# Eighteen more tiles turned by transposing transfers in a two-layer transformer trunk

## The chip, the cores and the metric

The kernel runs on one core of a Trainium2 chip. The metric is device time in microseconds (us) of one execution, as the median of several runs. One further execution was recorded by the profiler; all lines of the profile are from it.

## The reference

Two layers work on one residual stream `x` of 256 tokens by 2048 features, in f32. Layer 0 has differential attention, layer 1 multi-head latent attention. Each layer then attends into 256 memory tokens and applies a squared-ReLU MLP of width 8192:

```
mem_h = rms_norm(mem, mem_norm)
for i in range(2):
    h = rms_norm(x, attn_norm[i])
    x = x + (diff_attention(h) if i == 0 else mla_attention(h))
    x = x + memory_cross_attention(rms_norm(x, cross_norm[i]), mem_h, ...)
    x = x + square(relu(rms_norm(x, mlp_norm[i]) @ wup)) @ wdown
return rms_norm(x, final_norm)
```

Differential attention has 16 query and 16 key heads of 128 features, rotated in their first 32 features. Two softmaxes are subtracted for each of 8 pairs, the result weights values of 256 features, and each head's result is normed.

## The kernel before

**Tiles.** The 256 tokens are two row tiles (t = 0, 1) of 128 partitions. Features are handled in chunks of 512. TensorE contracts over partitions, so whatever enters a product as the stationary or contracted side must lie with features on partitions. Results come out with tokens on partitions. Between two products a 128x512 tile is therefore turned, as four 128x128 squares.

**Precision.** Every f32 operand is kept as a high and a low half (`hi`, and `lo = x - hi`), and each product is made of three matmuls: hi by hi, hi by lo, lo by hi. Weights arrive as 1 MB raw tiles (`raw_tile`, 7 buffers) by loads that SP issues in program order. ScalarE casts the high half (`whi`, L221), VectorE subtracts the low half (`wlo`, L222). One raw tile gives 24 matmuls. `take` keeps four raw tiles asked for ahead.

**Two ways to turn a tile.** On TensorE: `transpose4` calls `flip` (L174) four times into PSUM; `split` then makes the halves (ScalarE L366, VectorE L367). By transfers: `half_words` (L375) has ScalarE copy the 16-bit halves of the words into two planes (L377) and GpSimd (POOL) store them to DRAM (L379); `turned_by_dma` (L382) has SP issue a transposing transfer back into SBUF (L384), in program order with the weight loads; `split_landed` makes the halves from the tile that landed (L390, L391). Before the change the second way is used for MLP blocks 1 to 6 of each layer, four tiles a block, 48 in all.

**Order.** TensorE's order is written out by hand. Work beside the weight products (turning, softmax, scores) is written as generators, `Task`. A task yields a number: the time after which its next piece is due, by a clock that the program advances with each matmul that it emits (`mmul`, `flip`). `pump`, called behind every few matmuls, emits the pieces that are due. `need` emits whatever a product still waits for. So the constants T_EV to T_DMA, in us, say how long a piece is expected to take. ScalarE, VectorE and POOL get their order from a scheduler that simulates the timeline; `keep_in_program_order` ties single instructions to the written order: weight loads and transposing transfers on SP, accumulating loads on POOL, and the cast in `split_landed` on ScalarE.

**Differential attention.** `attention` goes through four groups of four heads. `project_diff(gi)` makes queries, keys and values of a group, each a chunk product of four raw tiles. `heads_T` (L568) evacuates queries or keys (L550), rotates them on POOL (`rope`, L561 to L566) and turns them. `attend_diff` is started when the group's values are made, and its pieces run under the next group's products; `normed` (L775) norms the weighted values, turns them and multiplies in the gains. For groups 0 and 1 the result goes into `dst.part`, from which the sums of a Strassen-like output product (`Pair`, WEAVE) are made before and during `project_diff(3)`. `mem_keys` (L1343) makes the keys of the memory tokens; they are turned by `heads_T` without rotation. After it come the last group's output product and the cross attention's query product.

**MLP.** Block 0's up product is made in two plain chunks, (0, 0) and (0, 1); blocks 1 to 7 use seven products instead of eight (`Seven`, p1 to p7), with weight sums made by VectorE (L868) or accumulating loads on POOL (L860). `out` (L1431) applies the squared ReLU and turns the tile. For blocks 1 to 6, the task of a block's last tile waits T_BATCH, issues the transposing transfers of the other three, waits on to T_STORE and issues its own. Blocks 0 and 7 are turned on TensorE. Down products follow between the up products; the last blocks' are in a closing stage.

`work` tiles with the tag `ev` (7 buffers) hold evacuated tiles, softmax rows, planes and landed tiles alike.

Of the kernel before, what the change touches and what calls it, by code (L numbers as in the profile page):

```python
# [10 lines left out]
F32 = mybir.dt.float32  # L11
# [16 lines left out]
LAST = MLP_BLOCKS - 1  # L28
# [3 lines left out]
WEAVE = "A1", "A2", "A5", "A3", "A6 B1", "A7 B2", "A4", "B5", "B3", "B6", "B7", "B4"  # L32
CLOSING = "u A1 u A2 B1 u A5 B2 u B5 u A6 u A3 B6 u B3 u A7 A4 u B7 u B4"

T_EV, T_TURN, T_ROT, T_SM, T_SQ, T_ADD, T_NORM, T_SUM, T_BATCH, T_STORE, T_LAND, T_DMA = 2.6, 2.6, 12.0, 6.5, 4.4, 2.2, 7.2, 3.0, 17.0, 22.0, 7.0, 8.0

URGENT = 250
NEG = -1.0e30
# [14 lines left out]
def trunk(ctx, tc, x, xT, xT0, mem, memT, positions, gcols, gfinal, lam_vecs, consts, W, out):  # L53
# [108 lines left out]
    def give_back():  # L162
        free_banks[0] += 1
# [218 lines left out]
    def turned_by_dma(there):  # L382
        landed = work.tile([P, 4, 2 * P], U16, tag="ev", name=nm("landed"), bufs=EVS)
        tc.keep_in_program_order(nc.sync.dma_start_transpose(landed, there))  # L384
        return landed.bitcast(F32)

    def split_landed(dst, t, src):
        at = slice(t * P, (t + 1) * P)
# [164 lines left out]
    def rope(view, cos, sin, heads, half):  # L553

        a, b = view[:, :, 0:half], view[:, :, half : 2 * half]
        c = cos.unsqueeze(1).broadcast_to([P, heads, half])
        s = sin.unsqueeze(1).broadcast_to([P, heads, half])
        m = [work.tile([P, heads, half], F32, tag=f"rope{i}", name=nm("rope"), padded_shape=[P, 4, 32], bufs=1) for i in range(2)]
        n = [work.tile([P, heads, half], F32, tag=f"rope{i + 2}", name=nm("rope"), padded_shape=[P, 4, 32], bufs=1) for i in range(2)]
        e = nc.gpsimd  # L560
        e.tensor_tensor(m[0], a, c, ALU.mult)  # L561
        e.tensor_tensor(m[1], b, s, ALU.mult)
        e.tensor_tensor(n[0], b, c, ALU.mult)
        e.tensor_tensor(n[1], a, s, ALU.mult)
        e.tensor_tensor(a, m[0], m[1], ALU.subtract)
        e.tensor_tensor(b, n[0], n[1], ALU.add)  # L566

    def heads_T(ps, t, scale, dst, rot=None, spare=False, given=None):  # L568


        def task():
            while given and not given():
                yield 0.5
            e = evacuate(ps, scale() if given else scale)
            if rot:
                cos, sin, heads, half = rot
                rope(e.rearrange("p (h d) -> p h d", h=heads), cos, sin, heads, half)
            yield T_ROT + (14.0 if given else 0.0) if rot else T_EV
            b = ps
            if spare:  # L580
                b = yield from side_bank()
            split(dst, t, transpose4(e, b))
            if spare:
                give_back()
            yield T_TURN

        dst.run(task())
# [152 lines left out]
    def attend_diff(q, k, v, dst, coef, subcols, slack=0.0):  # L740


        def block(t, heads, out):
            nk = (t + 1) * P
            sb = yield from side_bank()
            comps = [s for h in heads for s in (2 * h, 2 * h + 1)]
            scores(sb.rearrange("p (c k) -> p c k", k=nk), [whole(q, k, s, nk) for s in comps], t, True)
            n = 2 * len(heads)
            with urgent():
                pr, rs = softmax(sb, n)  # L750
                nc.vector.tensor_tensor(rs[:, :n], rs[:, :n], coef[:, :n], ALU.mult)
                a = work.tile([P, S], F32, tag="a", name=nm("a"))
                for i in range(len(heads)):
                    p0 = pr[:, 2 * i * nk : (2 * i + 1) * nk]
                    p1 = pr[:, (2 * i + 1) * nk : (2 * i + 2) * nk]
                    ai = a[:, i * nk : (i + 1) * nk]
                    nc.vector.tensor_scalar(ai, p1, rs[:, 2 * i + 1 : 2 * i + 2], None, ALU.mult)
                    nc.vector.scalar_tensor_tensor(ai, p0, rs[:, 2 * i : 2 * i + 1], ai, ALU.mult, ALU.add)
            yield T_SM + 6.3 + slack
            pT = prob_T(a, 2, sb)  # L760
            give_back()
            yield T_TURN + 1.6
            if not out:
                out.append((yield from side_bank()))
            po = out[0]
            nb = nk // P
            for i, h in enumerate(heads):
                for kb in range(nb):
                    blk = slice((i * nb + kb) * P, (i * nb + kb + 1) * P)
                    mm3(  # L770
                        po[:, h * S : (h + 1) * S], pT[:, 0, blk], pT[:, 1, blk],
                        val(v, 0, kb, h * S, S), val(v, 1, kb, h * S, S), kb == 0, kb == nb - 1,
                    )

        def normed(t, blocks, out):  # L775
            for b in blocks:
                yield b
            po = out[0]
            ss = small.tile([P, 2], F32, tag="ss2", name=nm("ss2"))
            for h in range(2):  # L780
                sum_squares(ss[:, h : h + 1], po[:, h * S : (h + 1) * S])
            r = rsqrt_mean(ss, 2, S)
            os = work.tile([P, CH], F32, tag="ev", name=nm("os"), bufs=EVS)
            nc.vector.tensor_tensor(
                os.rearrange("p (h d) -> p h d", h=2), po.rearrange("p (h d) -> p h d", h=2),
                r[:, 0:2].unsqueeze(2).broadcast_to([P, 2, S]), ALU.mult,
            )
            yield T_NORM + slack
            split(dst, t, scaled(transpose4(os, po), subcols, dst.part and dst.part(t)))
            give_back()  # L790
            yield T_TURN

        def task():
            for i in q.tasks + k.tasks:
                yield i
            out = [[], []]
            b0 = Task(block(0, (0, 1), out[0]))
            yield 4.0
            b1 = Task(block(1, (0,), out[1]))
            n0 = Task(normed(0, [b0], out[0]))  # L800
            yield 4.0
            b2 = Task(block(1, (1,), out[1]))
            yield Task(normed(1, [b1, b2], out[1]))
            yield n0

        dst.run(task())
# [514 lines left out]
    mem_rstd = []  # L1321
# [21 lines left out]
    def mem_keys(m):  # L1343
        mk = Held(unit())
        ps = matmul_chunk(m)
        for t in range(NT):
            heads_T(ps[t], t, mem_rstd[t], mk)
        return mk

    def mem_values(m):  # L1350
# [69 lines left out]
    def mlp(l, norm, gnext):  # L1420
# [10 lines left out]
        def out(b, c, t, src, r, wait):  # L1431

            if (b, c) not in hid:
                hid[b, c] = Held(unit())
            dst = hid[b, c]

            def task():
                nc.scalar.activation(r, src, AF.Relu, scale=rstd[t])  # L1438
                nc.scalar.activation(r, r, AF.Square)
                if 0 < b < LAST:  # L1440
                    mine = [half_words(r), None]
                    if (c, t) == (0, 1):
                        yield T_BATCH
                        for other in turning.pop(b):
                            other[1] = turned_by_dma(other[0])
                        yield T_STORE - T_BATCH
                        mine[1] = turned_by_dma(mine[0])
                    else:
                        turning.setdefault(b, []).append(mine)
                        while mine[1] is None:  # L1450
                            yield 0.7
                    yield T_LAND
                    split_landed(dst, t, mine[1])
                    yield T_DMA
                    return
                yield wait
                pt = yield from side_bank()
                pt = transpose4(r, pt)
                if b < LAST or (t, c) != (1, 0):
                    split(dst, t, pt)  # L1460
                if b == LAST:
                    pair.keep(t, c, pt)
                yield T_TURN
                give_back()

            dst.run(task())
# [76 lines left out]
    da_scales = []  # L1543
# [9 lines left out]
    def project_diff(gi):  # L1553
        q, k = Held(), Held()
        for i, dst in enumerate((q, k)):
            ps = matmul_chunk(acts, by_k=gi == i == 0)
            for t in range(NT):
                heads_T(
                    ps[t], t, (lambda i=i, t=t: da_scales[i][t]) if gi == 0 else da_scales[i][t], dst, (cos[:, t, :hd], sin[:, t, :hd], 4, hd),
                    spare=gi == 3, given=(lambda: da_scales) if gi == 0 else None,  # L1560
                )
        ps = matmul_chunk(acts)
        v = unit()
        for t in range(NT):
            values(ps[t], t, da_scales[1][t], v)
        return q, k, v
# [318 lines left out]
```

## Time and profile before

| | us |
|---|---|
| median of 3 runs | 2177.95 (2177.43 to 2177.97) |
| profiled execution, its own time | 2182.18 |
| its span | 2180.4 |
| TensorE busy | 2165.9 (99%) |
| VectorE busy | 1740.7 (80%) |
| ScalarE busy | 1452.7 (67%) |
| POOL busy | 205.4 (9%) |

The time includes 1.8 us around the span. PE is TensorE's matmul side, PEld its weight loads, DVE VectorE, ACT ScalarE, POOL GpSimd, SP the engine that issues most transfers. A name with q (SPq) is an engine's issuing side. In a group's row the columns are line, engine, operation, written tile <- read tiles, shape, count, then busy us and mean ns of one, then idle us before them with what ended it. In timelines and chains a row starts with its start and length in us; in square brackets stands the idle time before it.

### The profile page before, as it was taken

What the parts mean: (1) busy time and instruction counts of PE and PEld (TensorE: products, weight loads), DVE (VectorE), ACT (ScalarE), POOL (GpSimd) and SP (SyncE); (2) the same over time, 40 slices, a digit from 0 to 9 for tenths busy, and PEclk for the clock granted to TensorE, in tenths of its full rate; (3) what the DMA queues carried; (4) which work ended last, traced back from release to release, by engine and by line L of the source; (5) the groups of instructions that cost most, each with busy time, mean ns of one, the idle gap of its engine ahead of it and who ended that gap; (6) DMA issues with size and microseconds to landing.
All of it is one profiled execution on the core that took longest, in us unless ns stands there. A gap on an engine that the chain in (4) does not pass through costs nothing.

```text
span 2180.4 us, 27556 instructions
## 1 busy us (share of the span) xinstructions
PE 2165.9 (99%) x10259; PEld 1812.5 (83%) x10259; DVE 1740.7 (80%) x1962; ACT 1452.7 (67%) x1920; POOL 205.4 (9%) x318
## 2 busy tenths in 40 slices
PE   9999999999999999999999999999999999999998
PEld 7888888888888888887889988888888888888787
DVE  6665878679788889788886878778888888888887
ACT  7555656666767777776765755666777778677665
POOL 1112210001000000000000320000000000000001
PEclk9999999999999999999999999999999999999999
DMA  9446796448989999999996344635899999999895
GB/s 385 151 169 239 218 298 228 157 153 248 291 277 280 292 286 256 321 271 257 291 262 210 115 174 155 232 135 173 255 305 289 259 322 279 266 284 299 261 310 150
DMA packets 131414, 534.44 MB, mean 245 GB/s; under 512 B 60240, under 2 KB 60624, under 8 KB 72400
## 3 DMA queue, kind: packets, MB, share of 16 engines
q1 hardware_dynamic: 115488, 435.42, 56.0%
q0 software_dynamic: 15360, 96.48, 21.9%
q8 instruction: 80, 1.31, 0.2%
q10 hardware_dynamic: 432, 0.79, 0.1%
q14 instruction: 54, 0.44, 0.1%
HBM read 505.38 MB, written 14.68 MB: 239 GB/s over the span
## 4 chain that ended last, share of the span: by engine, by line
PE 96%; DVE 2%; DMA 1%; issue 1%; ACT 0%; DVEq 0%; POOLq 0%; POOL 0%
PE mm L170 63%; PE pr L170 29%; PE ax L170 3%; PE ax L174 1%; PE mm L174 1%; DMA raw<-in_mlp_wup_dram 1%; DVE wlo L222 1%; DVE unit L391 0%; ACT whi L221 0%; DVE x L545 0%; DMA raw<-in_xT_dram 0%; PE pr L174 0%; DVE p L671 0%; DVE raw L868 0%; DVE ev L1700 0%
## 5 line engine op out<-in xcount | busy, mean ns | idle before, releaser
L222 DVE TENSOR_TENSOR wlo<-raw,whi 128x1024 fp32r<-128x1024 f32 (+3 forms) x946 | 1139.2, 1215 | 351.8 <-ACT whi L221 329.4
L221 ACT CAST whi<-raw 128x1024 fp32r<-128x1024 f32 (+2 forms) x945 | 986.2, 1045 | 603.6 <-PE mm L170 449.0
L170 PE MATMUL mm<-whi,unit 128*128 128x512 f32 (+2 forms) x4000 | 1273.5, 389 | 0.8 <-ACT unit L1237 0.8
L170 PEld LDWEIGHTS mm<-whi,unit 128*128 128x128 f32 x4000 | 749.2, 188 | 148.7 <-ACT unit L1237 1.6
L170 PE MATMUL mm<-wlo,unit 128*128 128x512 f32 (+2 forms) x2000 | 773.8, 387 | 2.2 <-DVE wlo L222 1.9
L170 PE MATMUL pr<-whi,unit 128*128 128x512 f32 x1912 | 610.2, 389 | 0.0
L170 PEld LDWEIGHTS mm<-wlo,unit 128*128 128x128 f32 x2000 | 376.1, 188 | 76.0 <-DVE wlo L222 6.1
L170 PEld LDWEIGHTS pr<-whi,unit 128*128 128x128 f32 x1912 | 358.8, 188 | 73.7
L170 PE MATMUL pr<-wlo,unit 128*128 128x512 f32 x956 | 372.1, 389 | 1.2 <-DVE wlo L222 1.2
L170 PEld LDWEIGHTS pr<-wlo,unit 128*128 128x128 f32 x956 | 179.7, 188 | 40.5 <-DVE wlo L222 3.8
L868 DVE TENSOR_TENSOR raw<-raw,raw 128x2048 f32<-128x2048 f32 x40 | 91.4, 2286 | 6.3 <-DMA raw<-in_mlp_wup_dram 6.1
L545 DVE TENSOR_TENSOR x<-x,mm 128x512 f32<-128x512 f32 x128 | 84.8, 680 | 10.6 <-PE mm L170 10.5
L860 POOL DMA_DIRECT2D raw<-in_mlp_wup_dram x48 | 43.2, 900 | 498.2 <-DVE wlo L222 495.7
L431 POOL TENSOR_TENSOR rs<-rs,mhalf 128x1 f32<-128x1 f32 (+1 forms) x26 | 24.4, 944 | 599.1 <-DVE rs L430 599.1
L379 POOL DMA_DIRECT2D turned<-planes x48 | 27.2, 566 | 467.2 <-ACT planes L377 455.5
L222 DVE TENSOR_TENSOR wlo<-unit,whi 128x1024 fp32r<-128x1024 f32 x48 | 57.4, 1220 | 5.3 <-ACT whi L221 4.0
L221 ACT CAST whi<-unit 128x1024 fp32r<-128x1024 f32 x48 | 50.0, 1054 | 10.4 <-PE pr L170 10.4
L377 ACT COPY planes<-p 128x1024 uint16<-128x1024 uint16 x48 | 50.0, 1042 | 0.3
L170 PE MATMUL mm<-unit,whi 128*128 128x256 f32 x256 | 46.9, 284 | 0.0
L425 ACT ACTIVATE junk<-x 128x512 bf16<-128x512 f32 (+1 forms) x57 | 35.3, 620 | 9.6 <-DVE x L1073 5.2
L170 PEld LDWEIGHTS mm<-unit,whi 128*128 128x128 f32 x256 | 40.1, 192 | 0.3
L1438 ACT ACTIVATE p<-p,r 128x512 f32<-128x512 f32 x42 | 30.4, 724 | 13.9 <-DVE p L943 7.4
(195 smaller groups left out, 1275.6 us busy)
## 6 DMA issues: line engine op xcount, KB each, us to landing
raw<-in_mlp_wdown_dram SPq DMA_DIRECT2D x128, 1024.0 KB, 6.8
raw<-in_mlp_wup_dram SPq DMA_DIRECT2D x120, 1024.0 KB, 7.1
raw<-in_mlp_wup_dram POOLq DMA_DIRECT2D x48, 1024.0 KB, 8.9
raw<-in_da_wqkv_dram SPq DMA_DIRECT2D x45, 1024.0 KB, 7.6
raw<-in_da_wo_dram SPq DMA_DIRECT2D x16, 1024.0 KB, 7.1
raw<-in_ca_wkv_dram SPq DMA_DIRECT2D x16, 1024.0 KB, 4.9
raw<-in_mlp_wdown_dram POOLq DMA_DIRECT2D x16, 1024.0 KB, 10.2
raw<-in_mla_wo_dram SPq DMA_DIRECT2D x16, 1024.0 KB, 5.0
```

The lines of the kernel that those rows point to most:

```text
L170: return nc.tensor.matmul(o, stationary, moving, start=start, stop=stop, skip_group_check=onto)
L174: nc.tensor.transpose(o, src, ident)
L221: nc.scalar.copy(hi, r)
L222: nc.vector.tensor_tensor(lo, r, f32(hi), ALU.subtract)
L377: nc.scalar.copy(planes, src.bitcast(U16).rearrange("p (w s) -> p s w", s=2))
L379: nc.gpsimd.dma_start(there.rearrange("(q s) w -> q s w", s=2), planes)
L425: return nc.scalar.activation(junk[:, : src.shape[1]], src, AF.Square, scale=scale, accum_out=acc)
L431: nc.gpsimd.tensor_tensor(r[:, :n], r[:, :n], mhalf.broadcast_to([P, n]), ALU.pow)
L545: nc.vector.tensor_tensor(xc, xc, ps, ALU.add)
L860: tc.keep_in_program_order(nc.gpsimd.dma_start(onto, src, accum_op=ALU.add))
L868: nc.vector.tensor_tensor(o, o, q, ALU.add)
L1438: nc.scalar.activation(r, src, AF.Relu, scale=rstd[t])
```

## The change

Eighteen more tiles are turned by transfers instead of TensorE: queries and keys of group 1 and queries of group 2, weighted values of groups 0 and 1, memory keys of both layers, and the two tiles of block 0's first half in both layers. In `heads_T` the planes are made 3 us sooner than the flips were placed, the transposing transfer follows T_SHORT = 11 later, the split T_LAND = 7 after that, with `split` and not `split_landed`. In `normed` the PSUM bank is given back before the transfer. In block 0 each tile issues its own transfer T_STORE = 22 behind its store. For block 6 (LAST - 1) the batch of three is put 10 us later, and the fourth with it.

```
+T_SHORT = 11.0

 def turned_by_dma(there):
-        return landed.bitcast(F32)
+        return landed.bitcast(F32).rearrange("p k t -> p k t")

 def heads_T(..., by_dma=False):
+            if by_dma:
+                yield T_ROT - 3.0 if rot else 0.2
+                there = half_words(e)
+                yield T_SHORT
+                landed = turned_by_dma(there)
+                yield T_LAND
+                split(dst, t, landed)
+                yield T_TURN
+                return
             yield T_ROT + (14.0 if given else 0.0) if rot else T_EV

 def normed(t, blocks, out):
+            if dst.part:
+                yield T_NORM
+                give_back()
+                there = half_words(os)
+                yield T_SHORT
+                landed = turned_by_dma(there)
+                yield T_LAND
+                split(dst, t, scaled(landed, subcols, dst.part(t)))
+                yield T_TURN
+                return
             yield T_NORM + slack
-            split(dst, t, scaled(transpose4(os, po), subcols, dst.part and dst.part(t)))
+            split(dst, t, scaled(transpose4(os, po), subcols))

 def mem_keys(m):
-            heads_T(ps[t], t, mem_rstd[t], mk)
+            heads_T(ps[t], t, mem_rstd[t], mk, by_dma=True)

 def out(b, c, t, src, r, wait):
-                if 0 < b < LAST:
+                if b < LAST and (b, c) != (0, 1):
                     mine = [half_words(r), None]
-                    if (c, t) == (0, 1):
-                        yield T_BATCH
+                    if b == 0:
+                        yield T_STORE
+                        mine[1] = turned_by_dma(mine[0])
+                    elif (c, t) == (0, 1):
+                        yield T_BATCH + (10.0 if b == LAST - 1 else 0.0)

 def project_diff(gi):
-                    spare=gi == 3, given=(lambda: da_scales) if gi == 0 else None,
+                    spare=gi == 3, given=..., by_dma=gi == 1 or (gi, i) == (2, 0),
```

More of the change, by code (lines that the diff above doesn't have):

```diff
@@ L33 @@
 CLOSING = "u A1 u A2 B1 u A5 B2 u B5 u A6 u A3 B6 u B3 u A7 A4 u B7 u B4"
-T_EV, T_TURN, T_ROT, T_SM, T_SQ, T_ADD, T_NORM, T_SUM, T_BATCH, T_STORE, T_LAND, T_DMA = 2.6, 2.6, 12.0, 6.5, 4.4, 2.2, 7.2, 3.0, 17.0, 22.0, 7.0, 8.0
+T_EV, T_TURN, T_ROT, T_SM, T_SQ, T_ADD, T_NORM, T_SUM, T_BATCH, T_STORE, T_LAND, T_DMA, T_SHORT = 2.6, 2.6, 12.0, 6.5, 4.4, 2.2, 7.2, 3.0, 17.0, 22.0, 7.0, 8.0, 11.0
 URGENT = 250
@@ L566, in rope, with heads_T @@
         e.tensor_tensor(b, n[0], n[1], ALU.add)
-    def heads_T(ps, t, scale, dst, rot=None, spare=False, given=None):
+    def heads_T(ps, t, scale, dst, rot=None, spare=False, given=None, by_dma=False):
         def task():
@@ L1559, in project_diff @@
                     ps[t], t, (lambda i=i, t=t: da_scales[i][t]) if gi == 0 else da_scales[i][t], dst, (cos[:, t, :hd], sin[:, t, :hd], 4, hd),
-                    spare=gi == 3, given=(lambda: da_scales) if gi == 0 else None,
+                    spare=gi == 3, given=(lambda: da_scales) if gi == 0 else None, by_dma=gi == 1 or (gi, i) == (2, 0),
                 )
```

## The prediction

> **What bounds the kernel now.** I read the page first: busy time, the granted clock and the chain of work that ended last.
>
> ```profile
> span 2180.4 us, 27556 instructions
> PE 2165.9 (99%) x10259; PEld 1812.5 (83%) x10259; DVE 1740.7 (80%) x1962; ACT 1452.7 (67%) x1920; POOL 205.4 (9%) x318
> PE 96%; DVE 2%; DMA 1%; issue 1%; ACT 0%; DVEq 0%; POOLq 0%; POOL 0%
> PE mm L170 63%; PE pr L170 29%; PE ax L170 3%; PE ax L174 1%; PE mm L174 1%; DMA raw<-in_mlp_wup_dram 1%; DVE wlo L222 1%; DVE unit L391 0%; ACT whi L221 0%; DVE x L545 0%; DMA raw<-in_xT_dram 0%; PE pr L174 0%; DVE p L671 0%; DVE raw L868 0%; DVE ev L1700 0%
> ```
>
> TensorE works 2165.9 of 2180.4 us and is 96% of the chain. What it is given sets the time; everything else counts only where it makes TensorE wait. L174 is `flip`, the transposition of one 128x128 square by the identity. Each flip is TensorE's own work, on the chain, so taking one away shortens the program, if nothing new makes TensorE wait.
>
> Next the stretches in which the change acts (columns: us; busy time of PE, PEld, DVE, ACT, POOL; granted clock; DMA share; GB/s). They are, in order: groups 1 and 2 of differential attention, memory keys of layer 0, the first MLP block, the first batch of transposing transfers, and two stretches around block 6.
>
> ```profile
> 100.00:222.00 122.00, 122.00 (x597) 102.60 (x596) 74.30 (x101) 68.26 (x117) 24.23 (x51) 1.00 0.61 211
> 345.00:412.00 67.00, 67.00 (x331) 56.11 (x330) 54.47 (x84) 42.35 (x77) 1.42 (x2) 1.00 0.58 212
> 510.00:540.00 30.00, 30.00 (x138) 24.81 (x137) 26.93 (x23) 21.07 (x25) 0.87 (x1) 1.00 0.77 282
> 594.00:648.00 54.00, 54.00 (x240) 44.73 (x239) 46.80 (x40) 38.55 (x43) 2.91 (x4) 1.00 0.89 264
> 997.00:1001.00 4.00, 3.92 (x12) 3.12 (x13) 3.43 (x4) 0.00 (x0) 0.00 (x0) 0.66 1.23 227
> 2030.00:2060.00 30.00, 29.10 (x128) 23.19 (x127) 28.21 (x29) 21.52 (x26) 0.88 (x1) 1.00 0.83 244
> ```
>
> In the first three TensorE has no gap at all, the clock is full, ScalarE is at 56 to 70%, DMA at 58 to 77%. There is nothing to win there but TensorE's own work, and room beside it. Only the last two show time lost.
>
> **Flips removed.** Queries and keys of group 1 and queries of group 2: 3 products x 2 row tiles. Weighted values of groups 0 and 1: 2 x 2. Memory keys: 2 layers x 2. First half of block 0: 2 layers x 2. That is 6 + 4 + 4 + 4 = 18 tiles of four flips, 72 flips. The price of four is read from TensorE's timeline:
>
> ```profile
> 1035.40 0.39 PE L170 MATMUL pr<-wlo,unit 128*128 128x512 f32 x1
> 1035.63 0.39 PE L170 MATMUL pr<-whi,unit 128*128 128x512 f32 x1
> 1035.86 0.60 PE L174 MATMUL ax<-identr,p 128*128 128x128 f32 x4
> 1036.21 0.48 PE L170 MATMUL pr<-whi,unit 128*128 128x512 f32 x1
> 1036.53 0.40 PE L170 MATMUL pr<-wlo,unit 128*128 128x512 f32 x1
> ```
>
> Matmuls start 0.23 us apart (1035.40, 1035.63). From 1035.63 to 1036.53 are 0.90 us; two steps of 0.23 would have been 0.46. So four flips cost 0.44 us, and 18 x 0.44 = 7.9 us go. Nothing hides them: they lie in stretches without a gap.
>
> **What each tile gets instead**, from the tile views of the 48 transposing transfers there are (min/median/max) and the groups by shape:
>
> ```profile
> L377 ACT COPY planes<-p x48: 1037/1041/1047, 558.4 to 2003.5; 128x1024 uint16<-128x1024 uint16 x48
> DMA to landing us min/median/max: 2.9/6.2/9.6
> L384 SPq DMA_TRANSPOSE landed<-turned x48: 1226/2834/12801, 593.9 to 2016.8; - x48
> DMA to landing us min/median/max: 3.3/7.0/15.6
> L379 POOL DMA_DIRECT2D turned<-planes x48 | 27.2, 566 | 467.2 <-ACT planes L377 455.5 <-DMA raw<-in_mlp_wup_dram 11.7
> L366 ACT CAST unit<-mm 128x512 fp32r<-128x512 f32 x20 | 10.8, 586 | 2.2 <-PE mm L174 2.2
> L390 ACT CAST unit<-landed 128x512 fp32r<-128x512 f32 x48 | 27.3, 616 | 0.0
> ```
>
> ScalarE gains a copy of 1.04 us and casts in 0.62 instead of 0.59: 18 x 1.07 = 19.3 us in all, against 2180 - 1453 = 727 us that it stands idle. VectorE's work is the same. POOL issues 18 stores of 0.57 us = 10 us, in queue with the rotations; it is busy 24 of 122 us there. SP issues 18 transposing transfers, 1.2 to 12.8 us each. These are nought on the path as long as results come in time.
>
> *In time for TensorE?* Store plus transfer at the medians take 6.2 + 7.0 = 13.2 us (the schedule gives 11 + 7). TensorE's timeline shows where today's flips stand and who comes next:
>
> ```profile
> 137.44 1.03 PE L174 MATMUL mm<-identr,ev 128*128 128x128 f32 x8
> 149.20 1.45 PE L170 MATMUL ax<-unit,unit 128*128 128x128 f32 x12
> 211.18 1.03 PE L174 MATMUL mm<-identr,ev 128*128 128x128 f32 x8
> 222.95 1.45 PE L170 MATMUL ax<-unit,unit 128*128 128x128 f32 x12
> ```
>
> Keys of group 1 are flipped at 137.4 and used at 149.2. By the yields, today's flips stand 12 us behind the product and the new path ends 9 + 11 + 7 + 2.6 = 29.6 us behind it, that is at 137.4 - 12 + 29.6 = 155.0: the group's scores come some 6 us later. They are side work that TensorE's written order places between weight products, so they move and leave no hole. Queries of group 2 are needed only when that group's keys, still flipped at 211, are there. Weighted values feed the sums before `project_diff(3)`, memory keys feed scores after four products and the query product, and block 0's first half is first used by the down product behind its second half. No consumer stands right behind its transfer.
>
> *Held-up engines.* ScalarE's cast waits for the landing, and the weight casts queue behind it; VectorE's subtractions and TensorE wait for those. SP's transposing transfer waits for the store, and the weight loads queue behind it. The waits tell the cover:
>
> ```profile
> ACT whi L221 <- PE mm L170: 449.0, 368, 5.2
> SPq L189 <- DVE wlo L222: 1514.1, 316, 16.3
> 593.88 9.16 SPq L384 DMA_TRANSPOSE landed<-turned x2
> 978.27 0.33 SPq L189 DMA_DIRECT2D raw<-in_mlp_wup_dram  x1
> 978.70 15.61 SPq L384 DMA_TRANSPOSE landed<-turned  x3
> ```
>
> Weight casts wait for TensorE to free a buffer (up to 5.2 us), and loads wait for VectorE to free one (up to 16.3): both run ahead, so a delay under about 5 us on ScalarE or 16 on SP is covered. The batch at 593.88 held SP for 9.16 us, and 594 to 648 has no gap on TensorE. The new transfers go in ones and twos where DMA is no busier than that. I take 0.5 us for new waits, near zero as in that row; bounds 0 and, from the case below, 14. [...]
>
> **Sixth block later.** Its batch moves 10 us back in SP's order, past the next loads, up and down weights, and past nothing on POOL. The losses that it may touch:
>
> ```profile
> 978.27 15.24 DMA raw<-in_mlp_wup_dram
> 997.08 0.50 PE L170 MATMUL mm<-wlo,unit 128*128 128x512 f32 x1 [1.93 <-DVE wlo L222]
> 999.22 1.06 PE L170 MATMUL mm<-whi,unit 128*128 128x512 f32 x2
> 2038.05 1.89 DVE L391 TENSOR_TENSOR unit<-landed,unit 128x512 fp32r<-128x512 f32 x3
> 2042.16 2.29 DVE L868 TENSOR_TENSOR raw<-raw,raw 128x2048 f32<-128x2048 f32 x1 [1.09 <-DMA raw<-in_mlp_wup_dram]
> PE pr L170 <- DVE wlo L222: 1.2, 3, 0.8
> ```
>
> In layer 0 the load issued beside three transposing transfers took 15.24 us, TensorE waited 1.93 us, and then worked at a clock of 0.66 for 4 us (the window above), which is 0.34 x 4 = 1.4 more: 3.3 us. In layer 1 three landed tiles meet VectorE's addition; 2030 to 2060 has 0.9 us of TensorE gap. With the batch later, load and addition go first, and I expect both to go: 4.2 us of this execution. Bounds: 4.2 gained, or as much lost if the batch meets the next loads instead.
>
> **The sum**, against the profiled execution's own 2182.18 us (span 2180.4 and 1.8 around it): 2182.18 - 7.9 - 4.2 + 0.5 = 2170.6. It lies 4.2 us above the median of the runs, 2177.95. I take the stall in layer 0 for a mishap of this execution, since the same place in layer 1 has no such wait; the other runs have then little left to win there. So: 2177.95 - 7.9 - 0.5 (of the later batch) + 0.5 = 2170.0 us.
>
> **Rivals.**
> 1. *ScalarE stands at a late landing.* A landing of 15.6 us instead of 7.0 is 8.6 late; 5.2 are covered, 3.4 reach TensorE, and a slow clock as at 997 adds 1.4: 4.8 us each. Against it: the 48 casts from landed tiles waited 0.0 us. For it: the new casts of queries, keys and values, unlike those 48, aren't tied to the written order on ScalarE, and may be queued too soon. Two of the 18 eat the gain, three decide: 2170.0 + 14.4 = 2184.4, slower. Chance 0.12.
> 2. *SP holds the weights back at block 0,* where VectorE already is at 90% (26.93 of 30 us). Price as in layer 0 at 997, 3.3 us in both layers: 2176.6, no change that can be told. Chance 0.12.
> 3. *More is won:* the losses around block 6 are in every run. 2170.0 - 3.7 = 2166.3. Chance 0.18.
> 4. *The detour's length is exposed.* If the first consumer stood behind its transfer in the nine places, 13.2 us each less the 0.9 of two tiles' flips would add 9 x 12.3 = 111 us: 2281. Against it are the uses above. [...] Chance 0.01.
> The edit does what it says by the code: all 18 tiles take the new branch.
>
> **How the numbers follow.** The forecast has 0.57 and rival 3 has 0.18, both faster: 0.75. A measurement of this kernel can tell about 0.2%, 4.4 us, from no change; between 2173.6 and 2182.3 lies rival 2 with 0.12, above it rivals 1 and 4 with 0.13. The range leaves out the slow cases and the best end of rival 3: 2165.0 to 2178.5; the forecast's own is 2167 to 2173.
>
> **What would show it.** These groups of flips hold the 72:
>
> ```profile
> L174 PE MATMUL ax<-identr,ev 128*128 128x128 f32 x80 | 11.3, 274 | 0.7 <-DVE ev L1700 0.6
> L174 PE MATMUL mm<-identr,ev 128*128 128x128 f32 x80 | 10.4, 272 | 0.0
> L174 PE MATMUL ax<-identr,os 128*128 128x128 f32 x32 | 4.8, 272 | 0.0
> ```
>
> Right: they fall to 64, 40 and 16; 66 transposing transfers instead of 48; ScalarE up by about 19 us; no gap in TensorE from 100 to 222; no wait near 997 or 2045. Wrong: TensorE waiting for `wlo` behind a ScalarE cast from a landed tile (rival 1), late weight loads behind SP's transfers at 510 to 560 (rival 2), or a granted clock below 1.00 in a new place.

## The result, and the profile after

The changed kernel takes 2171.93 us in the median of ten runs (2170.76 to 2174.64). The kernel before, run beside it, takes 2178.02 (2177.43 to 2182.3). The ratio is 0.9971, with a 95% interval of 0.9962 to 0.9979: faster by 6.1 us, 0.29%. The profiled execution took 2170.76 us, the shortest of the ten, while the one profiled before, at 2182.18, was nearly as long as the longest run of its kernel. So the two traces lie 11.4 us apart where the medians lie 6.1.

The top of the page, and the group of stores:

```profile
span 2169.0 us, 27519 instructions
PE 2155.4 (99%) x10187; PEld 1805.5 (83%) x10187; DVE 1740.2 (80%) x1962; ACT 1465.6 (68%) x1938; POOL 221.0 (10%) x336
PE 95%; DVE 3%; DMA 1%; issue 1%; ACT 0%; DVEq 0%; POOLq 0%; POOL 0%
L379 POOL DMA_DIRECT2D turned<-planes x66 | 37.7, 572 | 673.5 <-ACT planes L377 661.2
```

TensorE has 72 matmuls fewer, and there are 66 stores instead of 48. ScalarE is busy 12.9 us more. The flips that are left, from TensorE's groups of L174 by shape (count, then ns min/median/max):

```profile
L174 PE MATMUL ax<-identr,ev x64: 270/273/329, 268.2 to 1575.7; 128*128 128x128 f32 x64
L174 PE MATMUL mm<-identr,ev x40: 270/273/273, 62.2 to 1449.2; 128*128 128x128 f32 x40
L174 PE MATMUL ax<-identr,os x16: 269/272/275, 250.9 to 371.8; 128*128 128x128 f32 x16
```

The windows of before, read again in the same places:

```profile
100.00:222.00 122.00, 122.00 (x582) 102.43 (x581) 79.03 (x101) 76.90 (x124) 31.06 (x57) 1.00 0.77 251
997.00:1001.00 4.00, 4.00 (x18) 3.28 (x18) 4.00 (x6) 2.11 (x2) 0.89 (x1) 1.00 0.82 260
2030.00:2060.00 30.00, 30.00 (x137) 24.75 (x136) 26.18 (x28) 23.54 (x29) 0.86 (x1) 1.00 0.89 277
```

Differential attention has no gap in spite of ScalarE's 77 busy us of 122 and DMA's 77% instead of 61%. The waits near 997 and 2045 are gone. New waits of TensorE, from its timeline:

```profile
155.51 1.45 PE L170 MATMUL ax<-unit,unit 128*128 128x128 f32 x12
548.67 0.74 PE L170 MATMUL mm<-whi,unit 128*128 128x512 f32 x2 [0.45 <-DVE unit L391]
1016.13 0.50 PE L170 MATMUL pr<-wlo,unit 128*128 128x512 f32 x1 [1.09 <-DVE wlo L222]
1568.43 0.50 PE L170 MATMUL mm<-whi,unit 128*128 128x512 f32 x1 [0.45 <-DVE unit L391]
```

The first row has no wait in brackets: group 1's scores, at 155.5. At 548.7 and 1568.4, block 0's first down products stand 0.45 us until VectorE has made the low half of a tile that has landed. The next matmul starts 0.61 us late, and with the slower starts behind it each wait costs about 0.7 us: in layer 0, four steps from 547.83 to 549.49 take 1.66 us instead of 0.91. The transfers are not what is late there. The two tiles of layer 0, from the view of landed tiles between 513 and 560 us:

```profile
L384 SPq DMA_TRANSPOSE landed<-turned x2: 1227/1730/2232, 513.8 to 521.0; - x2
L390 ACT CAST unit<-landed x2: 612/614/617, 546.0 to 546.6; 128x512 fp32r<-128x512 f32 x2
L391 DVE TENSOR_TENSOR unit<-landed,unit x2: 684/684/684, 547.9 to 548.5; 128x512 fp32r<-128x512 f32 x2
DMA to landing us min/median/max: 3.1/5.6/8.1
```

Both had landed by 529.1 at the latest (521.0 + 8.1), and ScalarE casts them 17 us after that without having waited for them. The casts stand where the written order has them, behind T_STORE and T_LAND, and on VectorE a sum of weights (L887) and a weight half go ahead of the low halves. In layer 1 the tiles had landed by 1547.8 and are cast at 1565.8.

The wait at 1016 is for an addition of two raw tiles on VectorE (L887, 2.29 us at 1012.65) that waited 2.28 us for a load. The waits of SP hold what is really new:

```profile
SPq L189 <- DVE wlo L222: 1403.0, 296, 16.3
SPq L384 <- DMA turned<-planes: 88.9, 12, 14.1
```

Before, SP never stood at a transposing transfer because its store had not landed. Now it does so 12 times, for 88.9 us in all, with every later weight load behind it.

### The profile page after: what moved, and what is told of

Its sections match the earlier page's. It is cut to its first block, busy times and chain, and to the rows that moved or that the text cites. A ratio compares the mean times of both kernels' runs of the same rounds, so it can differ in the third digit from the quotient of the medians.

```text
span 2169.0 us, 27519 instructions
## 1 busy us (share of the span) xinstructions
PE 2155.4 (99%) x10187; PEld 1805.5 (83%) x10187; DVE 1740.2 (80%) x1962; ACT 1465.6 (68%) x1938; POOL 221.0 (10%) x336
## 4 chain that ended last, share of the span: by engine, by line
PE 95%; DVE 3%; DMA 1%; issue 1%; ACT 0%; DVEq 0%; POOLq 0%; POOL 0%
PE mm L170 62%; PE pr L170 28%; PE ax L170 3%; DVE wlo L222 1%; DMA raw<-in_mlp_wup_dram 1%; PE ax L174 1%; PE mm L174 1%; DVE raw L887 0%; DVE unit L391 0%; ACT whi L221 0%; DVE x L545 0%; DMA raw<-in_da_wqkv_dram 0%; PE pr L174 0%; DVE p L680 0%; DVE ev L1722 0%
## 5 line engine op out<-in xcount | busy, mean ns | idle before, releaser
L379 POOL DMA_DIRECT2D turned<-planes x66 | 37.7, 572 | 673.5 <-ACT planes L377 661.2
L887 DVE TENSOR_TENSOR raw<-raw,raw 128x2048 f32<-128x2048 f32 x40 | 91.5, 2288 | 8.8 <-DMA raw<-in_mlp_wup_dram 8.6
L545 DVE TENSOR_TENSOR x<-x,mm 128x512 f32<-128x512 f32 x128 | 85.3, 682 | 14.1 <-PE mm L170 14.0
L431 POOL TENSOR_TENSOR rs<-rs,mhalf 128x1 f32<-128x1 f32 (+1 forms) x26 | 24.9, 962 | 408.1 <-DVE rs L430 408.0
```

Source lines behind the costliest of these rows:

```text
L379: nc.gpsimd.dma_start(there.rearrange("(q s) w -> q s w", s=2), planes)
L431: nc.gpsimd.tensor_tensor(r[:, :n], r[:, :n], mhalf.broadcast_to([P, n]), ALU.pow)
L545: nc.vector.tensor_tensor(xc, xc, ps, ALU.add)
L887: nc.vector.tensor_tensor(o, o, q, ALU.add)
```

## The experiments

Each kernel was timed in five rounds beside the kernel before. Half the width of an interval is about 0.1%, some 2 us.

**The later batch alone** (the kernel before with this one edit):

```
-                        yield T_BATCH
+                        yield T_BATCH + (10.0 if b == LAST - 1 else 0.0)
```

> The kernel before with nothing but block 6's batch put 10 us later; all 72 flips stay. Theory A (the long wait near 997 us and its slow clock were a mishap of one execution, so there is little to win here): 2177.5 us, within 1 us of the kernel before. Theory B (those losses are in every run): 2174.3 us. Either way no wait of 1.9 us near 997; a new wait of about 1.2 us on VectorE's addition may stand near 1020, as in the changed kernel.

2177.83 us against 2178.31, ratio 0.9998 (0.9989 to 1.0007). Putting the batch later is worth nothing that these runs can tell.

**The flips alone** (the change with the batch of block 6 where it was):

```
-                        yield T_BATCH + (10.0 if b == LAST - 1 else 0.0)
+                        yield T_BATCH
```

> The changed kernel with block 6's batch put back: only the 18 tiles are moved. Theory A: the 72 flips are nearly all of the gain, 2172.4 us (0.5 above the changed kernel). Theory B: the later batch earned a good part of it, 2175 us or more, with a wait of 1 to 2 us and a slow clock near 990.

2171.36 us, ratio 0.9968 (0.9956 to 0.9981): all of the gain. Its profile has no wait near 997 or 2045 either. So their absence in the changed kernel, which the prediction names as a sign, says nothing about the later batch.

**Differential attention's ten tiles back on TensorE:**

```
-                    spare=gi == 3, given=..., by_dma=gi == 1 or (gi, i) == (2, 0),
+                    spare=gi == 3, given=..., by_dma=False,
 def normed(t, blocks, out):
-            if dst.part:
+            if False:
...
-            split(dst, t, scaled(transpose4(os, po), subcols))
+            split(dst, t, scaled(transpose4(os, po), subcols, dst.part and dst.part(t)))
```

> The changed kernel with the ten tiles of differential attention (queries, keys, weighted values) turned on TensorE again; memory keys, block 0 and block 6 stay changed. Theory A (each tile is worth its four flips, 0.44 us, and nothing else): 2171.9 + 4.4 = 2176.3 us. Theory E (moving these ten also costs: the memory rows' loads stand behind the transposing transfers on SP, and on POOL the first accumulating load of the output weights stands behind the memory norms): less than that, 2174.5 to 2175.5, runs within 1 us of each other, and the first accumulating load near 219 us instead of 230.

2176.1 us, ratio 0.9988 (0.9979 to 0.9997): 4.2 us of the gain gone with ten tiles by the medians, 3.7 by the ratios: 0.37 to 0.42 a tile, close to the price of four flips. The two intervals just touch, at 0.9979.

**Block 0's four tiles back on TensorE:**

```
-                if b < LAST and (b, c) != (0, 1):
+                if 0 < b < LAST:
```

> Block 0's first half is flipped on TensorE again in both layers; the other 14 tiles go by transfer. Theory A (each tile is worth its four flips, 0.42 us): 1.7 us slower than the change, 2173.6. Theory B (block 0's tiles arrive just late and take back in waits and slow matmuls, 0.6 us and more in each layer, what their flips had cost): 2171 to 2172.2, no difference, and a spread nearer to the 0.9 us of the kernel before than to the change's 3.9.

2171.14 us, ratio 0.9965 (0.9952 to 0.9977). Fourteen tiles give as much as eighteen: block 0's four bring nothing that can be told. Its waits at 549 and 1568 are gone, and 1.8 us of flips are back. The spread doesn't decide anything: the kernel before itself ran from 2177.27 to 2182.57 beside it.

**Block 0's transfers sooner:**

```
                     if b == 0:
-                        yield T_STORE
+                        yield T_SHORT
```

> The changed kernel, but block 0's two tiles issue their transfers 11 us behind their stores instead of 22. The profile of the changed kernel has two waits of 0.45 us on VectorE's subtraction from block 0's landed tile (548.7 and 1568.4 us), 0.61 us each with the slower steps around them. Theory C (part of the missing gain is that these tiles come just too late): both waits go, 2170.7 us. Theory D (part of it is that SP stands at the transposing transfer until the store has landed, and weight loads stand behind it): SP stands longer, no gain, 2172 to 2174 us.

2170.94 us, ratio 0.9971 (0.996 to 0.9981). The two waits of 0.45 us go, and one of 0.54 comes at 532.5. What takes them away is not the transfers themselves, of which in layer 0 the first is issued no sooner than in the change (514.3) and the second 4.7 us sooner (516.3). The pieces behind them in the written order move too: the first cast stands at 536.3 instead of 546.0, and again waits for no landing. One us less than the change in the median, which these runs can't tell from none.

**The wait between store and transfer, 16 us and 4 us instead of 11:**

```
-... T_SHORT = ..., 8.0, 11.0
+... T_SHORT = ..., 8.0, 16.0     (second kernel: 4.0)
```

> The changed kernel with T_SHORT 16 instead of 11: the transposing transfers of queries, keys, weighted values and memory keys stand 5 us later in SP's order, behind more weight loads. In the changed kernel SP stands 88.9 us in 12 waits for stores. Theory D (SP's standing costs time): those waits fall under 50 us, the time to about 2171 us and the runs lie within 2 us of each other. Theory C (only block 0's late tiles and block 6 cost): no change, 2171.9 us.

> The changed kernel with T_SHORT 4 instead of 11: the transposing transfers stand 7 us sooner in SP's order, so SP reaches them before their stores have landed. Theory D (SP's standing costs time): SP waits over 120 us for stores instead of 89, weights for the products at 130 to 150 us arrive too late, TensorE waits some us there: 2175 us or more. Theory E (what matters is only that the memory rows are loaded in time): SP stands longer, but the lead of the weights covers it, the memory rows come sooner: 2171 us.

Both lose the whole gain: 2180.49 us with 16, ratio 1.001 (1.0001 to 1.0019), and 2179.94 with 4, ratio 1.0005 (0.9996 to 1.0014). I had not expected that of 16. With 16, the chain that ended last leaves TensorE at 217 us and comes back to it at 250, by way of POOL. Part of it (start and length of each piece in us):

```profile
222.35 2.09 POOL rs L431
224.44 13.29 issue
...
237.76 0.07 POOL rs L431
...
238.58 8.96 DMA raw<-in_da_wo_dram
247.54 0.02 issue
247.57 1.05 ACT whi L221
```

The timelines of POOL and TensorE, and SP's waits from 199 to 219 us, of the same kernel:

```profile
237.76 0.56 POOL L431 TENSOR_TENSOR rs<-rs,mhalf 128x1 f32<-128x1 f32 x1 [13.32 <-DVE rs L430]
238.58 0.94 POOL L1003 DMA_DIRECT2D raw<-in_da_wo_dram  x1 [0.26 <-issue]
248.66 0.80 PE L170 MATMUL pr<-whi,unit 128*128 128x512 f32 x1 [6.14 <-ACT whi L221]
SPq L189 <- DVE unit L372: 8.4, 2, 7.9
```

From the cause on: SP's loads of the memory rows stand 7.9 us until VectorE (L372) has read a landed tile of weighted values, for both use the seven `ev` buffers. The rows are late, and the second memory norm on POOL (L431), which waits 13.3 us, comes at 237.8 instead of 229.7. Where these 8.1 us arise show ScalarE's last square of a memory row and VectorE's step before POOL's, first with 16 us and then in the change:

```profile
230.41 0.65 ACT L425 ACTIVATE junk<-memrow 128x512 bf16<-128x512 f32 x1
237.54 0.14 DVE L430 TENSOR_SCALAR rs<-tot 128x1 f32<-128x1 f32 x1
226.61 0.64 ACT L425 ACTIVATE junk<-memrow 128x512 bf16<-128x512 f32 x1
229.45 0.15 DVE L430 TENSOR_SCALAR rs<-tot 128x1 f32<-128x1 f32 x1
```

The rows account for 3.8 of them. The other 4.3 are added on VectorE, which works without a pause and has three weight halves and parts of a softmax in its order before this step. Behind the norm in POOL's order stands the first accumulating load of the output weights (one that adds to what is in its raw tile). The cast of that tile stands on ScalarE, the casts behind it too, and TensorE waits 6.1 us. Then it runs slowly. Granted clock (the column before the last two) of 240 to 256 us, with 16 us and in the change, and below them the two stretches behind the wait with 16 us:

```profile
240.00:256.00 16.00, 9.39 (x38) 7.21 (x38) 8.29 (x11) 7.32 (x12) 1.63 (x2) 0.79 0.72 162
240.00:256.00 16.00, 16.00 (x85) 13.68 (x84) 14.07 (x20) 11.66 (x21) 4.57 (x7) 1.00 0.89 268
248.00:252.00 4.00, 2.87 (x6) 2.00 (x7) 3.36 (x3) 3.45 (x4) 0.56 (x1) 0.50 0.12 49
252.00:256.00 4.00, 4.00 (x18) 3.32 (x18) 3.33 (x5) 2.32 (x3) 0.35 (x1) 0.72 0.76 125
```

The chain is read from one trace of each kernel. Only its part from the memory norm on was put to a test, in the runs with the norm one group sooner below.

With 4 us the same load is issued at 235.1, ScalarE's cast stands for it, and TensorE waits 2.88 us at 245.7. In the change it is issued at 230.4, 11 us later than before the change, and ScalarE's cast waits 3.1 us for it. TensorE doesn't, yet: the change sits just short of this edge.

**The memory rows' norm one group sooner,** with 11, 16 and 4 us:

```
-lambda gi: mem_norm() if gi == 1 else None
+lambda gi: mem_norm() if gi == 0 else None
```

> The changed kernel with the memory rows' loads and norms placed behind project_diff(1) instead of project_diff(2), so that they stand neither behind the last transposing transfers on SP nor before the accumulating loads on POOL. Theory E: the first accumulating load is issued near 219 us instead of 230, the runs' spread of 4 us shrinks to about 1, median 2170.8 us. Theory C (only block 0's late tiles cost): no change, 2171.9 us.

> The wait of 16 us with the memory rows' norm one group sooner (gi == 0). Theory G (the 8.5 us that the wait of 16 costs are one chain: late memory rows, memory norm on POOL, the accumulating load of da_wo queued behind it, the weight cast behind that, 6.1 us of TensorE and the slow clock after it): the accumulating load is issued near 203 us instead of 238.6, the wait of 6.14 us at 248.7 is gone, the clock from 240 to 256 is 1.00, and the time is 2170.5 to 2173. Theory H (longer waits are worse in themselves, since every consumer comes 5 us later): the time stays within 2 us of the 2180.5 of the wait of 16.

> The wait of 4 us with the memory rows' norm one group sooner. Theory G (the same chain as with 16 us): the wait of 2.88 us at 245.7 and the half clock after it go, about 5 us, and the time falls from 2179.9 to about 2175; block 0's first half is still used late (1.7 and 1.0 us). Theory H' (SyncE stands at the stores, 118 us in all with the wait of 4, and weights come late everywhere): at most 2 us are won, 2178 or more.

With 11 us: 2171.86, ratio 0.9972 (0.9961 to 0.9982), the time of the change, although the accumulating load now leaves at 202.8. So the edge costs the change nothing. With 16: 2175.46, ratio 0.9982 (0.9974 to 0.9991); the load leaves at 203.7, the wait of 6.1 us is gone, and 5.0 of the 8.6 us over the changed kernel come back, not all. What is left has waits of its own, in TensorE's timeline:

```profile
243.24 0.44 PE L174 MATMUL ax<-identr,a 128*128 128x128 f32 x2 [2.02 <-DVE a L767]
553.41 0.50 PE L170 MATMUL mm<-whi,unit 128*128 128x512 f32 x1 [1.15 <-DVE unit L391]
```

With 4: 2172.15, ratio 0.9968 (0.9956 to 0.998); 7.8 us of 8.0 come back, more than I expected. So the loss of the short wait went with the place of the norm. The trace with 4 us, of an execution 2.0 us under the median, shows about 5 us of it: waits of 2.88 and 0.77 us, and a clock of 0.59 from 248 to 252. And SP's waits for stores in the kernel with 4 us and the rows sooner are as long as with 4 us alone (117.7 us):

```profile
SPq L384 <- DMA turned<-planes: 117.6, 12, 22.4
```

SP stands 117.6 us at stores that have not landed, up to 22.4 at a time, in a kernel that is as fast as the changed one. Standing SP alone costs nothing here.

**Cross attention's queries by transfer too,** 22 tiles:

```
-            heads_T(ps[t], t, rq[t], q)
+            heads_T(ps[t], t, rq[t], q, by_dma=True)
```

> The changed kernel with the cross attention's queries (four tiles more, two in each layer) turned by transfers too. Here the consumer stands close: the scores need the queries, and the output product needs the attention, with one product of 22 us between. Theory A alone: 16 flips fewer, 2171.9 - 1.8 = 2170.1 us. Theory of the exposed detour (the prediction's rival 4, at one place): the queries come 15.6 us later, and most of it shows as a gap in TensorE before the output product, 8 to 13 us and a slow clock in each layer: 2187 to 2197 us.

2182.69 us, ratio 1.0018 (1.0009 to 1.0027): 10.8 us slower than the change. Two rows of TensorE's timeline:

```profile
454.06 1.23 PE L174 MATMUL ax<-identr,p 128*128 128x128 f32 x8 [3.18 <-DVE p L680]
1480.15 0.45 PE L174 MATMUL ax<-identr,p 128*128 128x128 f32 x1 [3.17 <-DVE p L680]
```

Queries that come later bring the scores and the softmax (L680) so close to the flips of its result that TensorE stands 3.18 us in each layer. In the changed kernel those flips lie four at a time between weight products from 440.7 on, without a wait. The two waits are 6.4 us. The clock behind them, which is 1.00 in the same stretches of the change:

```profile
456.00:460.00 4.00, 4.00 (x23) 3.80 (x22) 2.53 (x4) 1.17 (x2) 0.00 (x0) 0.63 0.02 4
1478.00:1482.00 4.00, 1.85 (x9) 1.89 (x10) 4.00 (x12) 2.52 (x10) 0.00 (x0) 0.70 0.01 2
1482.00:1486.00 4.00, 3.58 (x25) 3.27 (x23) 2.62 (x5) 1.69 (x3) 0.00 (x0) 0.88 0.01 4
```

Busy time times what is missing from 1.00 gives another 2.5 us, so these two places hold 8.9 us. The loss is 10.8 by the medians, and the profiled execution, of 2185.3 us, was the longest of its kernel. It has other waits further on, the longest 1.94 us at 1894, which I did not trace back.

**Both edges moved:** memory rows one group sooner and block 0's transfers after T_SHORT.

> The change with memory rows one group sooner and block 0's transfers issued 11 us instead of T_STORE's after their stores' schedule point, as in the two runs that had one of these each (2171.86 and 2170.94). If both edges cost something: 2169.5 to 2170.5, faster than the change by 1.4 us or more. If neither does: 2171 to 2172.

2170.85 us (2169.88 to 2172.37), ratio 0.9962 (0.9949 to 0.9974). The lowest median of all, by 1.1 us under the change; that is within what these runs can't tell from none.

## Why the prediction was right, and where it was not

Predicted 2170.0 us, measured 2171.93; the cause that it named, flips that leave TensorE, is the one the runs show.

- **Flips removed: right.** The counts fell to 64, 40 and 16 as predicted. By the starts, four flips in the changed kernel still cost 0.447 us. The flips alone give the whole gain, and ten tiles put back cost 0.37 to 0.42 us each.
- **Results in time: right for fourteen tiles, wrong for block 0's four.** Group 1's scores came at 155.5 (predicted 155.0). But block 0's first half, "first used by the down product behind its second half", was used just as its halves were made: two waits of about 0.7 us, 1.5 us back, of 4 x 0.45 = 1.8 won. What failed there is not the time of store and transfer, which the prediction reckoned, since the tiles had lain landed for 17 us. It is the place of the halves in the written order, which it did not look at for these tiles. Without these four tiles the time was no longer.
- **New waits, 0.5 us: mis-sized.** 2177.95 less 18 x 0.447 would be 2169.9; the median lies 2.0 above it. 1.5 are block 0's two waits. The profile has a wait of 1.09 us at 1016 as well, but the flips alone had none there. Where the last 0.5 us lie is open, and less than these runs resolve.
- **The later batch: wrong in its mechanism, small in the sum.** I gave it 4.2 us of the profiled execution and 0.5 of the runs. The runs show no gain from it, though they can't tell 0.5 us from nothing, and the waits near 997 and 2045 are gone without it as well. That the wait of 1.93 us at 997 was a mishap of one execution, as the prediction took it to be, fits this; no second trace of the kernel before shows it. Rival 3 had the losses in every run, 3.7 us more to win, and the later batch alone, at 0.5 us under the kernel before, speaks against it.
- **Held-up engines: the cover held, but the account left out POOL.** I priced SP by a transposing transfer's own 1.2 to 12.8 us. The larger part is the wait for the store, 88.9 us in all, which I knew to be possible and did not size. It lies under the cover, as the run with 117.6 us shows. On SP a transposing transfer took longer than a plain load: in the change 1.63 us in the median of 66, and the eight loads of memory rows, of the same 256 KB, 0.39. To the landing the two lie close: 6.0 us against 6.5, and before the change, with 48 transposing transfers, 7.0 against 5.8. What the prediction did not see is the second way out of SP's queue: memory rows, POOL's norm, the accumulating load behind it. The change moved that load by 11 us without harm; with waits of 4 and 16 it goes 4.7 and 8.1 us later still, and the gain is lost. Nothing in the prediction's account tells 11 us from 4 or 16, so that the forecast held in this point is luck.
- **ScalarE.** Its eighteen new copies take 18.4 us by their groups, as priced; its busy time rose by 12.9 of the 19 predicted. Of the difference, 1.1 us are weight casts that took less in all. Summed by groups the rise is 16.9 us (1524.1 to 1541.0); that the other 4.0 are records that overlap, which busy time counts once, is my estimate. It stands idle for 703 us.
- **Rivals 1 and 2** did not come. ScalarE's 52 casts in `split_landed` waited 0.0 us. Of the new tiles that rival 1 meant, the ten casts on ScalarE waited 0.0 us too, and the four reads by VectorE (L372) 0.5 us, once. At block 0, TensorE waited for the landed tile's halves, not for weights. Rival 4, the exposed detour, is what the cross queries do when they are added: 10.8 us slower with these four tiles, where the eighteen are 6.1 us faster. In this kernel a flip on TensorE was the better way where the result is waited for, not where TensorE is the bound and the detour is covered.

## What to carry to other kernels

When TensorE is 99% busy, take off it whatever another path can do in time, and count the gain by what TensorE's stream gets shorter; the longer path cost nothing here where no consumer stood behind it (the ten tiles of differential attention won 0.37 to 0.42 us each) and 10.8 us where one did. Then check each consumer by its own row, since four tiles whose halves were made half a microsecond late, long after they had landed, were worth nothing that can be told among fourteen that paid. Follow an in-order queue past the first engine: with the wait of 16 us the delay ran from a landed tile's buffer (7.9 us) over SP's loads, VectorE's order, POOL's norm (8.1 us later than in the change) and POOL's next load to TensorE (6.1 us), and POOL, in its middle, is busy for 10% of the span in the change.

## What I had not expected of the hardware

- Stands of SP, which issues the weight loads, left the time as it was: 2171.93 us with 12 of them, 88.9 us in all and 14.1 at most, and 2172.15 with 12 of 117.6 us in all and 22.4 at most.
- With T_SHORT 16, TensorE's wait cost more than its length. After the 6.14 us idle that ended at 248.7, the clock was 0.50 to 252 and 0.72 to 256, on 2.87 and 4.00 busy us: 1.4 + 1.1 = 2.5 us more. With a second wait of 0.46 us that is 9.1 us, against 8.6 that the runs lost to the change.
- Eight loads of 256 KB held SP for 7.0 us in the change, 12.9 with T_SHORT 16 and 15.2 with 4: their size is the same in all three, and one load alone took 0.33 to 0.39 us of SP in the median. With 16, 7.9 of the 12.9 us are one wait for a buffer.
